# Three tiles' state-space output, gate and norm moved into the last attention blocks of an encoder-layer kernel

## The chip, the cores and the metric

The kernel runs on one core of a Trainium2 chip: one TensorE (PE), one VectorE (DVE), one ScalarE (ACT), one GpSimd (POOL), and DMA queues that are issued from SyncE (SP). Each engine works off its own queue in order and waits on semaphores for the others. The metric is the device time of one execution in microseconds (us), as the median of the runs.

## The reference

One layer of a hybrid encoder over a prompt of 2048 tokens and a sample of 256, model width 1024, fp32. What the change touches is the mixing of the two groups of heads:

```python
h = rms_norm(x, attn_norm_g)
q_lat, kv_lat, z, xbc, dt_raw = jnp.split(h @ w_in, IN_SPLITS, axis=-1)
mla_out = rms_norm(mla_mixer(q_lat, kv_lat, ...), attn_out_norm_g)   # 8 heads of attention, width 512
...
y = y_fwd + y_bwd + xs * d_skip                    # SSD: forward and backward chunked scan
y = y.reshape(b, s, SSD_WIDTH) * jax.nn.silu(z)    # gate, width 512
ssd_out = rms_norm(y, ssd_norm_g)
...
x = x + jnp.concatenate([mla_out, ssd_out], axis=-1) @ w_out
h = rms_norm(x, ffn_norm_g)
return x + (jax.nn.silu(h @ w_gate) * (h @ w_up)) @ w_down
```

## The kernel before

The tokens lie in 18 tiles of 128: tiles 0 to 15 are the prompt, 16 and 17 the sample. fp32 products are made of three matmuls with values split into a high and a low part: `mm3` (L115 to L117). A split takes two operations: the high part on ScalarE or GpSimd (weights: L123 or L121; banks: L130), the low part on VectorE (L126, L131).

The stages follow each other: input projections, conv and SSD scans (up to some 676 us), attention (to some 1549), output projection with the norms (`gather`, `turned`, `project`, to some 1800), a feed-forward part with up and gate, and the down projection.

Attention goes through a list `work` of blocks: 8 heads, and in each head the prompt's four blocks of 4 query tiles and one block of the sample. A block makes scores for its query tiles (L115 to L117), row maxima (`tensor_reduce`, L739, and L767 over the chunks) and exponentials (L748), and puts its key tiles on a list `turn`. While the next block makes its scores, these key tiles are turned (four transposes, L781, into a bank of the ring `ta`, `ta`, `tb`), split from the bank to SBUF (`pT`, L130 and L131) and multiplied with v (L789, L790). The block's result is turned back (L796, L808, L810, L811) and scaled into `mla` on GpSimd (L812). PE, ACT, DVE and POOL keep the order in which the code is written here (`manual_schedule`). After the last block only its remaining key tiles are left, the tail. Keys and values of even heads lie in pool `c_kv0`, of odd heads in `c_kv1`; SyncE's loads are ordered by the scheduler.

The output projection then goes through the tiles in falling order, 15 to 0, then 17, 16. `gather` adds the backward scan's state to the SSD output: state scaled on GpSimd (L896), summed on VectorE (L897), two matmuls (L902), product with the decay (L904), sum on GpSimd (L905); for the last tile of a sequence this falls away. Then come the gate (L908), two squares on ScalarE (L911, L912), a `rsqrt` of eleven small dependent operations on VectorE (L141 to L146) and two scalings (L914, L915). `turned` turns the tile (L923) and splits it (`mT`, L130, L131); `project` multiplies it with the eight output weights `wo0` to `wo7`, which are loaded and split (`load_wo`) at the third tile.

## Time and profile before

| | |
|---|---|
| median of 3 runs | 3298.39 us (3298.23 to 3300.56) |
| profiled execution | 3295.84 us, its span 3294.1 us |
| mean granted TensorE clock | 0.987 |
| busy share of the span | TensorE 97%, VectorE 71%, ScalarE 52%, GpSimd 9% |

A row of a timeline gives the start and the length of a run of equal instructions; the bracket at its end is the time in which the engine stood idle ahead of it, and what ended that. The ends of matmuls are modelled and overlap; the distance between two starts is the safer measure. The granted clock of 1.00 is 2.4 GHz, 0.50 is 1.2 GHz, and what lies between is a window with both.

### The profile page before, as it was taken

Reading aid. Unit: us, or ns where it says so; the run is one execution under the profiler, and the core shown is the slowest. Engines: PE = TensorE matmul, PEld = TensorE weight load, DVE = VectorE, ACT = ScalarE, POOL = GpSimd, SP = SyncE. Lnnn points to the kernel's source line nnn. Section 1 sums busy time; section 2 is a strip of 40 time slices with the busy share of each in tenths; the row PEclk is TensorE's granted clock in tenths of the full one; section 3 lists DMA queues with packets and bytes.
Section 4 is the critical chain, followed back from the end, with each engine's and each line's share of the span. In section 5 each row is a group of like instructions: output and inputs, shape, how many; then the busy total and the mean of one; then the engine's idle time right before and its main releaser. Section 6 shows DMA issues by size and latency. Waiting matters only on the chain.

```text
span 3294.1 us, 48707 instructions
## 1 busy us (share of the span) xinstructions
PE 3198.0 (97%) x17834; PEld 2855.6 (87%) x17834; DVE 2330.8 (71%) x4390; ACT 1707.7 (52%) x3578; POOL 306.9 (9%) x382
## 2 busy tenths in 40 slices
PE   7999999889999999998999999999999999999998
PEld 6888999878888888886788999999999999788887
DVE  5545677778888888888684777787778776344576
ACT  5454554567777777776322455445444444322233
POOL 2121133411111110001120000000000000000000
PEclk9999999999999999999999999999999999999999
DMA  8556422423323332102453333333333333554664
GB/s 299 206 203 205 154 103 101 125 78 92 87 64 89 94 87 61 45 20 86 132 170 121 110 132 125 144 110 127 127 143 107 121 123 123 159 154 151 185 194 138
DMA packets 263823, 419.43 MB, mean 127 GB/s; under 512 B 23392, under 2 KB 175744, under 8 KB 260960
## 3 DMA queue, kind: packets, MB, share of 16 engines
q1 hardware_dynamic: 263584, 416.31, 38.3%
q8 instruction: 141, 2.31, 0.3%
q14 instruction: 98, 0.80, 0.1%
HBM read 274.57 MB, written 145.65 MB: 128 GB/s over the span
## 4 chain that ended last, share of the span: by engine, by line
PE 81%; DVE 4%; DMA 2%; ACT 2%; issue 1%; POOL 0%; ACTq 0%; DVEq 0%; SPq 0%
PE bank_mb L1073 8%; PE bank_ma L1073 8%; PE bank_ta L1073 8%; PE bank_ma L117 7%; PE bank_ma L115 7%; PE bank_ma L116 7%; PE bank_mb L115 5%; PE bank_mb L117 5%; PE bank_mb L116 5%; PE bank_ta L781 4%; PE bank_o L789 3%; PE bank_o L790 3%; PE bank_tb L781 2%; PE bank_tb L1073 2%; PE bank_o L1073 2%; DVE Y L470 1%
## 5 line engine op out<-in xcount | busy, mean ns | idle before, releaser
L1006 DVE TENSOR_TENSOR ws<-rawf,ws 128x512 fp32r<-128x512 f32 x396 | 267.7, 688 | 100.5 <-ACT ws L1005 98.8
L1005 ACT ACTIVATE ws<-rawf 128x512 fp32r<-128x512 f32 x396 | 241.9, 627 | 178.4 <-PE bank_tb L1073 38.1
L1073 PE MATMUL bank_mb<-U,ws 128*128 128x384 f32 x1584 | 303.0, 336 | 2.3 <-ACT c L1082 2.2
L1073 PE MATMUL bank_ma<-U,ws 128*128 128x384 f32 x1584 | 300.8, 337 | 2.6 <-ACT U L1005 2.1
L1073 PE MATMUL bank_ta<-U,ws 128*128 128x384 f32 x1584 | 297.8, 335 | 3.7 <-ACT U L1005 2.4
L131 DVE TENSOR_TENSOR pT<-bank_ta,pT 128x512 fp32r<-128x512 f32 (+1 forms) x352 | 239.6, 681 | 62.3 <-ACT pT L130 52.5
L1073 PEld LDWEIGHTS bank_ta<-U,ws 128*128 128x128 f32 x1584 | 276.5, 188 | 5.4 <-ACT U L1005 2.9
L1073 PEld LDWEIGHTS bank_ma<-U,ws 128*128 128x128 f32 x1584 | 277.4, 189 | 3.6 <-ACT U L1005 2.4
L1073 PEld LDWEIGHTS bank_mb<-U,ws 128*128 128x128 f32 x1584 | 276.2, 188 | 4.0 <-ACT c L1082 3.9
L130 ACT ACTIVATE pT<-bank_ta 128x512 fp32r<-128x512 f32 (+1 forms) x352 | 209.1, 596 | 117.3 <-PE bank_ta L781 116.6
L789 PE MATMUL bank_o<-pT,v 128*128 128x512 f32 x528 | 249.5, 473 | 1.9 <-ACT ot L796 1.9
L781 PEld LDWEIGHTS bank_ta<-ident,pr 128*128 128x128 f32 x1388 | 171.4, 141 | 48.6 <-DVE pT L131 7.7
L781 PE MATMUL bank_ta<-ident,pr 128*128 128x128 f32 x1388 | 211.2, 274 | 2.0 <-DVE pT L131 2.0
L739 DVE TENSOR_REDUCE mx<-bank_ma 128x1 f32<-128x512 f32 (+1 forms) x261 | 177.0, 678 | 50.4 <-PE bank_ma L117 50.0
L790 PE MATMUL bank_o<-pT,v 128*128 128x512 f32 x528 | 206.8, 392 | 0.0
L1194 ACT ACTIVATE as<-rawa 128x1408 fp32r<-128x1408 f32 x63 | 86.9, 1379 | 225.2 <-PE bank_ma L117 118.1
L470 DVE SCALAR_TENSOR_TENSOR Y<-X,cw,Y 128x256 f32<-128x256 f32 x288 | 172.6, 661 | 27.6 <-ACT X L457 27.3
L748 ACT ACTIVATE pr<-bank_mb,mx 128x512 f32<-128x512 f32 (+1 forms) x261 | 181.4, 695 | 8.4 <-DVE mx L739 4.8
L748 ACT ACTIVATE pr<-bank_ma,mx 128x512 f32<-128x512 f32 (+1 forms) x261 | 179.1, 686 | 6.0 <-DVE mx L767 5.1
L739 DVE TENSOR_REDUCE mx<-bank_mb 128x1 f32<-128x512 f32 (+1 forms) x261 | 176.8, 677 | 7.2 <-PE bank_mb L117 3.6
L115 PE MATMUL bank_ma<-hT,wx 128*128 128x256 f32 x576 | 163.2, 284 | 2.1 <-POOL wx L121 1.5
L116 PE MATMUL bank_ma<-hT,wx 128*128 128x256 f32 x576 | 162.7, 283 | 0.0
...
## 6 DMA issues: line engine op xcount, KB each, us to landing
...
```

The lines of the kernel that those rows point to most:

```text
L115: nc.tensor.matmul(ps, wh, xh, start=start, stop=False)
L116: nc.tensor.matmul(ps, wh, xl, start=False, stop=False)
L117: nc.tensor.matmul(ps, wl, xh, start=False, stop=stop)
L131: nc.vector.tensor_tensor(lo, ps, f(hi), op=ALU.subtract)
L739: nc.vector.tensor_reduce(mx[:, j:j + 1], ps[:, :m * P], axis=AX.X, op=ALU.max, negate=nch == 1)
L748: nc.scalar.activation(e[:, :m * P], ps[:, :m * P], AF.Exp, bias=bias, accum_out=rs[:, i, j:j + 1])
L781: nc.tensor.transpose(ps[:, i * P:(i + 1) * P], pr[i, kt // 4][:, kt % 4 * P:(kt % 4 + 1) * P], ident)
L789: nc.tensor.matmul(po[0][:, :n], v[:, s0 + kt, :], pT[:, 0, :n], start=kt == 0, stop=False)
L790: nc.tensor.matmul(po[0][:, :n], v[:, s0 + kt, :], pT[:, 1, :n], start=False, stop=kt == sn - 1)
L1005: nc.scalar.activation(dst[:, 0], src, AF.Copy)
L1006: nc.vector.tensor_tensor(dst[:, 1], src, f(dst)[:, 0], op=ALU.subtract)
L1073: nc.tensor.matmul(ps[:, :W], w[:, a, k, :], x[:, b, k, :], start=k + n == 0 and not more, stop=k == HK - 1 and n == 2, skip_group_check=more)
```

## The change

- The blocks of the last head are worked off backwards: prompt tiles 12 to 15 first, then 8, 4 and 0, then the sample's block.
- `gather` is cut in two: `ssd_out` (SSD output, gate and its square) and `gather` (attention's square, rsqrt, two scalings). For tiles 15, 14 and 13 both stand in attention's code: `ssd_out` of 15 after block 4, of 14 after block 0 with `gather` of 15 behind it, of 13 after the sample's block with `gather` of 14 and 13 behind it. Then follow the tail's key tiles.
- Their buffers, and those of all later tiles, are slices of the tiles that held the even heads' keys and values (`mixk`, `mixv`), since the last head is an odd one. There are 3 y, 2 z, 2 state terms, 2 states (before: 4, 2, 3, 2). A unit of the output matmuls goes to a bank of the ring `t` instead of `o`.
- `wo0` is loaded and split when three blocks are left. `wo1` to `wo7` are loaded ahead of the projection's loop, which begins at its third step.
- The pool `c_kv0` and two small ones are opened ahead of attention's other pools.

The diff, without blank lines and without the body of the old `gather` (its operations are those of `ssd_out` and `gather`):

```diff
                 nc.sync.dma_start(d_B[m][:, j], out)
+    G = 3
+    W = G * P
+    assert NT % (2 * G) == 0
+    order = [c for c, _ in falling(1)]
+    parts = [(order[i:i + G], order[i + G:i + 2 * G]) for i in range(0, NT, 2 * G)]
+    kv0 = pool(mixer, "c_kv0", 1)
+    small = pool(mixer, "d_s", 2)
+    w0p = pool(mixer, "d_w0", 1)
+    ends = {a + m - 1 for a, m in seq_tiles}
+    bst, wo, mix = {}, {}, {}
+    def load_wo(k, home):
+        wo[k] = home.tile([P, 2, D], F32R, name=f"wo{k}")
+        raw = op.tile([P, D], F32, name="o", tag="o")
+        nc.sync.dma_start(raw, io["w_out"][:, k, :])
+        split_w(wo[k][:, 0], wo[k][:, 1], raw, "pool" if k % 2 else "act")
+    def mix_tiles():
+        a = kv0.tile([P, 9, SW], F32, name="mixk", tag="k")
+        b = kv0.tile([P, NT * P], F32, name="mixv", tag="v")
+        mix["y"], mix["z"], mix["sc"] = ([a[:, i, :] for i in r] for r in ((0, 1, 2), (3, 4), (5, 6)))
+        mix["g"] = a[:, 7], a[:, 8]
+        mix["nsb"], mix["to"] = ([b[:, i * SW:(i + 1) * SW] for i in r] for r in ((0, 1), (2,)))
+        mix["ct"] = [b[:, 3 * SW + i * NG * P:3 * SW + (i + 1) * NG * P] for i in range(2)]
+        nc.sync.dma_start(mix["g"][0], io["mix_g"][:, :SW].to_broadcast([P, SW]))
+        nc.sync.dma_start(mix["g"][1], io["mix_g"][:, SW:].to_broadcast([P, SW]))
+    def nxt(name):
+        mix[name].append(mix[name].pop(0))
+        return mix[name][-1]
+    def hbd(a, c):
+        return a[:, 1, c, :].rearrange("p (h o) -> p h o", o=1).to_broadcast([P, SH, SP])
+    def by_head(a):
+        return a.rearrange("p (h d) -> p h d", h=SH)
+    def ssd_out(c):
+        y, z, sc = nxt("y"), nxt("z"), nxt("sc")
+        nc.sync.dma_start(y, d_y[c])
+        nc.sync.dma_start(z, d_z[c])
+        nc.sync.dma_start(sc, d_sb[c])
+        if c not in ends:
+            ct = nxt("ct")
+            nc.sync.dma_start(ct, d_C[c])
+            old = bst["s"]
+            ns = nxt("nsb")
+            nc.gpsimd.tensor_tensor(by_head(ns), by_head(old), hbd(dec, c), op=ALU.mult)
+            nc.vector.tensor_tensor(ns, ns, sc, op=ALU.add)
+            bst["s"] = ns
+            po = bank("t")
+            for g in range(NG):
+                s = slice(g * 256, (g + 1) * 256)
+                nc.tensor.matmul(po[:, s], ct[:, g * P:(g + 1) * P], old[:, s], start=True, stop=True)
+            to = nxt("to")
+            nc.vector.tensor_tensor(by_head(to), by_head(po), hbd(dfs, c), op=ALU.mult)
+            nc.gpsimd.tensor_tensor(y, y, to, op=ALU.add)
+        else:
+            bst["s"] = sc
+        nc.vector.tensor_tensor(y, y, z, op=ALU.mult)
+        ss = small.tile([P, 16], F32, name="ss2", tag="ss2")
+        nc.scalar.activation(z, y, AF.Square, accum_out=ss[:, 1:2])
+        return y, z, ss
+    def gather(c, y, z, ss):
+        nc.scalar.activation(z, mla[c][:, 0, :], AF.Square, accum_out=ss[:, 0:1])
+        r = rsqrt(small, ss[:, :2], 2, SW, "m")
+        nc.vector.scalar_tensor_tensor(mla[c][:, 0, :], mla[c][:, 0, :], r[:, 0:1], mix["g"][0], op0=ALU.mult, op1=ALU.mult)
+        nc.vector.scalar_tensor_tensor(y, y, r[:, 1:2], mix["g"][1], op0=ALU.mult, op1=ALU.mult)
+        return y
     with ExitStack() as ph:
-        kvs = [pool(ph, "c_kv0", 1)]
+        kvs = [kv0]
         qp = pool(ph, "c_q", 2)
         lp = pool(ph, "c_l", 2)
         sb = pool(ph, "c_sb", 2)
@@ -814,7 +891,8 @@
             for kt in range(sn):
                 turn.append(lambda kt=kt: turned(kt))
-        work = [(h, s0 + o, min(4, sn - o), s0, sn) for h in range(NH) for s0, sn in seq_tiles for o in range(0, sn, 4)]
+        work = [(h, s0 + o, min(4, sn - o), s0, sn) for h in range(NH) for s0, sn in seq_tiles for o in list(range(0, sn, 4))[::-1 if h == NH - 1 else 1]]
         heads = {}
         def next_block():
@@ -826,24 +904,29 @@
         next_block()
         sums = block_sums()
         with tc.manual_schedule(engines={mybir.EngineType.PE, mybir.EngineType.Activation, mybir.EngineType.DVE, mybir.EngineType.Pool}):
+            ys = {}
             while work:
                 next_block()
                 for _ in range(2):
                     next(sums, None)
-            for _ in sums:
-                pass
+                if len(work) == 3:
+                    for _ in sums:
+                        pass
+                    mix_tiles()
+                    load_wo(0, w0p)
+                if len(work) < 3:
+                    ys[2 - len(work)] = ssd_out(order[2 - len(work)])
+                if len(work) == 1:
+                    ys[0] = gather(order[0], *ys[0])
+            for i in (1, 2):
+                ys[i] = gather(order[i], *ys[i])
             while tail:
                 tail.popleft()()
             while turn or prod or late:
                 step()
-    G = 3
-    W = G * P
-    assert NT % (2 * G) == 0
-    order = [c for c, _ in falling(1)]
-    parts = [(order[i:i + G], order[i + G:i + 2 * G]) for i in range(0, NT, 2 * G)]
     hbs = [pool(ctx, "e_hb0", 1, side="right")]
     H, first_xs = {}, {}
@@ -861,59 +944,6 @@
         sb = pool(ph, "d_sb", 2)
         wp = pool(ph, "d_w", 1)
         mp = pool(ph, "d_m", 2)
-        wo = [wp.tile([P, 2, D], F32R, name=f"wo{k}") for k in range(KD)]
-        def load_wo(k):
-            raw = op.tile([P, D], F32, name="o", tag="o")
-            nc.sync.dma_start(raw, io["w_out"][:, k, :])
-            split_w(wo[k][:, 0], wo[k][:, 1], raw, "pool" if k % 2 else "act")
-        grow = wp.tile([P, D], F32, name="grow")
-        nc.sync.dma_start(grow, io["mix_g"].to_broadcast([P, D]))
...
         def turned(c, y):
             mT = mp.tile([P, 2, KD, P], F32R, name="mT", tag="mT", bufs=3)
@@ -944,13 +974,12 @@
             if c == order[G]:
                 columns_of(0, 0, [first_xs.pop(t) for t in order[:G]])
-        ys, mTs = {}, {}
-        WO = {2: range(KD)}
-        for i in range(NT + 3):
-            if i < NT:
-                ys[i] = gather(order[i])
-            for k in WO.get(i, ()):
-                load_wo(k)
+        mTs = {}
+        for k in range(1, KD):
+            load_wo(k, wp)
+        for i in range(2, NT + 3):
+            if 2 < i < NT:
+                ys[i] = gather(order[i], *ssd_out(order[i]))
             if 0 <= i - 2 < NT:
                 mTs[i - 2] = turned(order[i - 2], ys.pop(i - 2))
             if 0 <= i - 3 < NT:
```

How it moves instructions, at three places. In the changed kernel L816 is the reduction of scores, L858 the transposes of key tiles, L866 and L867 the products, L888 the turning back, L738, L740, L744 the output matmuls, decay product and gate, L753 and L754 the scalings, L953 the transposes of `turned`.

VectorE, before, in attention's last key tiles (`nsb` is the state of the scan):

```order
L131 TENSOR_TENSOR pT<-bank_ta,pT 128x512
L897 TENSOR_TENSOR nsb<-nsb,sc 128x512
L131 TENSOR_TENSOR pT<-bank_ta,pT 128x512
L802 TENSOR_REDUCE ri<-rs 128x4
L803 RECIPROCAL ri<-ri 128x4
L811 TENSOR_TENSOR lo<-bank_tb,lo 128x256
L131 TENSOR_TENSOR pT<-bank_ta,pT 128x512
L897 TENSOR_TENSOR nsb<-nsb,sc 128x512
```

VectorE in the changed kernel, at the same place: the step with `ssd_out` of tile 14 and `gather` of tile 15.

```order
L131 TENSOR_TENSOR pT<-bank_tb,pT 128x512
L131 TENSOR_TENSOR pT<-bank_ta,pT 128x512
L733 TENSOR_TENSOR mixv<-mixv,mixk 128x512
L740 TENSOR_TENSOR mixv<-bank_tb,dfs 128x512
L744 TENSOR_TENSOR mixk<-mixk 128x512
L141 TENSOR_SCALAR rs_ms<-ss_16956 128x2
...
L144 SCALAR_TENSOR_TENSOR rs_u<-rs_y 128x2
L145 TENSOR_TENSOR rs_u<-rs_u,rs_ms 128x2
L146 SCALAR_TENSOR_TENSOR rs_y<-rs_u,rs_y 128x2
L753 SCALAR_TENSOR_TENSOR mla_7376<-mla_7376,rs_y,mixk 128x512
L754 SCALAR_TENSOR_TENSOR mixk<-mixk,rs_y 128x512
L816 TENSOR_REDUCE mx<-bank_ma 128x1
L131 TENSOR_TENSOR pT<-bank_ta,pT 128x512 x3
```

Eleven small operations (three are shown ahead of the scalings), a decay product, a gate and two scalings now stand in one piece between the split of one key tile and that of the next.

VectorE, before, a few rows after attention's last product, where the first gates and weight splits stand (`wo_17501` is `wo0`, the next are `wo1` to `wo3`):

```order
L908 TENSOR_TENSOR y_17538<-y_17538,z_17539 128x512
L144 SCALAR_TENSOR_TENSOR rs_u<-rs_y 128x2
L904 TENSOR_TENSOR to_17590<-bank_o,dfs 128x512
L145 TENSOR_TENSOR rs_u<-rs_u,rs_ms 128x2
L897 TENSOR_TENSOR nsb<-nsb,sc 128x512
L126 TENSOR_TENSOR wo_17501<-o,wo_17501 128x1024
L146 SCALAR_TENSOR_TENSOR rs_y<-rs_u,rs_y 128x2
L126 TENSOR_TENSOR wo_17502<-o,wo_17502 128x1024
L126 TENSOR_TENSOR wo_17503<-o,wo_17503 128x1024
L126 TENSOR_TENSOR wo_17504<-o,wo_17504 128x1024
```

VectorE in the changed kernel, after attention's last product (`wo_17600` is `wo1`, then `wo2`, `wo4`, `wo3`):

```order
L888 TENSOR_TENSOR lo<-bank_tb,lo 128x256
L882 RECIPROCAL ri<-rs 128x2
L888 TENSOR_TENSOR lo<-bank_ta,lo 128x128
L740 TENSOR_TENSOR mixv<-bank_ta,dfs 128x512
L126 TENSOR_TENSOR wo_17600<-o,wo_17600 128x1024
L126 TENSOR_TENSOR wo_17605<-o,wo_17605 128x1024
L126 TENSOR_TENSOR wo_17615<-o,wo_17615 128x1024
L126 TENSOR_TENSOR wo_17610<-o,wo_17610 128x1024
L131 TENSOR_TENSOR mT<-bank_ta,mT 128x512
L131 TENSOR_TENSOR mT<-bank_tb,mT 128x512
```

Four weight splits now stand in a row ahead of the first split of `mT`, and the gates and rsqrt of the first tiles are gone from here.

TensorE, before, at the end of the SSD part (L588 updates states, L601 makes diagonal outputs; the rows with k and q are scores of attention's first block):

```order
L115 MATMUL bank_mb<-k,q 128x512
L116 MATMUL bank_mb<-k,q 128x512
L117 MATMUL bank_mb<-k,q 128x512
L588 MATMUL bank_tb<-xd_7214,bt 128x256 x2
L115 MATMUL bank_ta<-k,q 128x512
...
L588 MATMUL bank_tb<-xd_7285,bt 128x256 x2
L601 MATMUL bank_o<-xs,e_7248 128x64 x7
L580 MATMUL bank_tb<-ns_7291,Y 128x256 x2
L588 MATMUL bank_tb<-xd_7326,bt 128x256 x2
L588 MATMUL bank_tb<-xd_7328,bt 128x256 x2
L115 MATMUL bank_tb<-k,q 128x512
```

TensorE in the changed kernel, at the same place:

```order
L588 MATMUL bank_tb<-xd_7214,bt 128x256 x2
L601 MATMUL bank_o<-xs,e_7165 128x64 x8
L588 MATMUL bank_tb<-xd_7216,bt 128x256 x2
L588 MATMUL bank_tb<-xd_7283,bt 128x256 x2
L601 MATMUL bank_o<-xs,e_7248 128x64
L588 MATMUL bank_tb<-xd_7285,bt 128x256 x2
L601 MATMUL bank_o<-xs,e_7248 128x64 x7
L580 MATMUL bank_tb<-ns_7291,Y 128x256 x2
L588 MATMUL bank_tb<-xd_7326,bt 128x256 x2
L588 MATMUL bank_tb<-xd_7328,bt 128x256 x2
L115 MATMUL bank_ma<-k,q 128x512
L116 MATMUL bank_ma<-k,q 128x512
```

The score groups that stood between the SSD part's matmuls now stand behind the last of them. On SyncE's queue the first q load moved likewise from ahead of the last stores of the scan to behind `d_sb_168`.

## Rows read from the trace of the kernel before

**Rows 1.** The page's busy time of each engine over the whole span: us, share of the span, instructions.

```profile
PE 3198.0 (97%) x17834; PEld 2855.6 (87%) x17834; DVE 2330.8 (71%) x4390; ACT 1707.7 (52%) x3578; POOL 306.9 (9%) x382
```

**Rows 2.** Windows by stage, core 0: start and end, length, then busy us (instructions) of TensorE, its weight loads, VectorE, ScalarE and GpSimd, the granted clock, the DMA share and GB/s. Attention ends shortly before 1550; the output projection fills 1600 to 1700.

```profile
1400.00:1500.00 100.00, 99.27 (x562) 81.24 (x561) 82.90 (x151) 76.90 (x193) 2.85 (x5) 1.00 0.06 17
1530.00:1540.00 10.00, 8.76 (x58) 7.03 (x57) 8.78 (x17) 7.97 (x20) 1.66 (x2) 1.00 0.36 120
1550.00:1560.00 10.00, 4.15 (x14) 2.41 (x12) 9.00 (x15) 4.37 (x10) 7.00 (x8) 0.75 0.51 159
1560.00:1570.00 10.00, 2.05 (x5) 1.18 (x5) 9.88 (x17) 2.39 (x5) 4.33 (x4) 0.50 0.99 350
1570.00:1580.00 10.00, 7.89 (x24) 5.87 (x25) 10.00 (x17) 3.36 (x7) 4.14 (x4) 0.55 0.36 112
1590.00:1600.00 10.00, 8.97 (x44) 6.94 (x43) 9.90 (x35) 3.93 (x10) 3.06 (x3) 1.00 0.57 172
1600.00:1700.00 100.00, 100.00 (x488) 83.81 (x487) 69.95 (x206) 26.85 (x58) 14.61 (x12) 1.00 0.45 147
```

**Rows 3.** Timeline of TensorE at the join of attention and output projection: start, us, instruction, and in brackets the idle time ahead of it and what ended that.

```profile
1549.07 1.07 PE L808 MATMUL bank_ta<-ident,ot 128*128 128x128 f32 x6
1549.98 1.03 PE L902 MATMUL bank_o<-sc,ct 128*128 128x256 f32 x4
...
1557.85 2.04 PE L902 MATMUL bank_o<-nsb,ct 128*128 128x256 f32 x4 [4.91 <-DVE rs_u L145]
1567.29 2.05 PE L902 MATMUL bank_o<-nsb,ct 128*128 128x256 f32 x4 [7.39 <-DVE rs_u L144]
1570.00 1.11 PE L923 MATMUL bank_tb<-ident,mla 128*128 128x128 f32 x4 [0.66 <-DVE mla L914]
...
1572.28 0.78 PE L115 MATMUL bank_ma<-wo,mT 128*128 128x512 f32 x1
...
1577.50 0.99 PE L117 MATMUL bank_ma<-wo,mT 128*128 128x512 f32 x1
...
1579.27 0.39 PE L115 MATMUL bank_ma<-wo,mT 128*128 128x512 f32 x1
```

**Rows 4.** Timeline of VectorE at the same join.

```profile
1551.05 0.69 DVE L904 TENSOR_TENSOR to<-bank_o,dfs 128x512 f32<-128x512 f32 x1 [0.37 <-PE bank_o L902]
1551.66 0.28 DVE L811 TENSOR_TENSOR lo<-bank_ta,lo 128x128 f32<-128x128 f32 x1
...
1553.51 0.96 DVE L144 SCALAR_TENSOR_TENSOR rs_u<-rs_y 128x2 f32<-128x2 f32 x1
...
1556.40 0.68 DVE L908 TENSOR_TENSOR y<-y,z 128x512 f32<-128x512 f32 x1
...
1558.34 2.29 DVE L126 TENSOR_TENSOR wo<-o,wo 128x1024 fp32r<-128x1024 f32 x1
...
1561.47 3.48 DVE L126 TENSOR_TENSOR wo<-o,wo 128x1024 fp32r<-128x1024 f32 x3
```

**Rows 5.** Timeline of VectorE a little later, with GpSimd idle from 1590.5: the end of one rsqrt and the two scalings behind it.

```profile
1590.55 0.16 DVE L144 SCALAR_TENSOR_TENSOR rs_u<-rs_y 128x2 f32<-128x2 f32 x1
1590.74 0.16 DVE L145 TENSOR_TENSOR rs_u<-rs_u,rs_ms 128x2 f32<-128x2 f32 x1
...
1591.14 0.75 DVE L914 SCALAR_TENSOR_TENSOR mla<-mla,rs_y,grow 128x512 f32<-128x512 f32 x1
1591.81 0.75 DVE L915 SCALAR_TENSOR_TENSOR y<-y,rs_y,grow 128x512 f32<-128x512 f32 x1
```

**Rows 6.** Timeline of ScalarE at the join: the two squares of one tile.

```profile
1565.79 0.63 ACT L911 ACTIVATE junk<-y 128x512 f32<-128x512 f32 x1 [7.14 <-DVE y L908]
...
1566.54 0.63 ACT L912 ACTIVATE junk<-mla 128x512 f32<-128x512 f32 x1
```

**Rows 7.** Timeline of GpSimd at the join.

```profile
1551.82 1.27 POOL L905 TENSOR_TENSOR y<-y,to 128x512 f32<-128x512 f32 x1 [0.52 <-DVE to L904]
...
1553.41 1.04 POOL L896 TENSOR_TENSOR nsb<-nsb,dec 128x512 f32<-128x512 f32 x1
1554.43 2.04 POOL L121 TENSOR_SCALAR wo<-o 128x1024 fp32r<-128x1024 f32 x2
```

**Rows 8.** Timeline of VectorE in attention's last key tiles.

```profile
1543.00 0.69 DVE L131 TENSOR_TENSOR pT<-bank_ta,pT 128x512 fp32r<-128x512 f32 x1 [0.21 <-ACT pT L130]
```

**Rows 9.** Timeline of TensorE from the end of the SSD part into attention.

```profile
674.72 1.10 PE L588 MATMUL bank_tb<-xd,bt 128*128 128x256 f32 x4 [0.94 <-DVE ns L592]
...
680.28 0.50 PE L115 MATMUL bank_ma<-k,q 96*128 96x512 f32 x1 [2.76 <-ACT pr L748]
...
681.39 0.63 PE L116 MATMUL bank_mb<-k,q 96*128 96x512 f32 x1
...
684.73 0.40 PE L115 MATMUL bank_ta<-k,q 96*128 96x512 f32 x1
684.97 0.40 PE L116 MATMUL bank_ta<-k,q 96*128 96x512 f32 x1
```

**Rows 10.** Timeline of VectorE in the same place: the first of the seven reductions and the row maximum.

```profile
675.09 0.68 DVE L739 TENSOR_REDUCE mx<-bank_ma 128x1 f32<-128x512 f32 x1
...
679.27 0.14 DVE L767 TENSOR_REDUCE mx<-mx 128x1 f32<-128x4 f32 x1
```

**Rows 11.** Timeline of SyncE's queue there: the store that waits.

```profile
666.24 4.16 SPq L598 DMA_DIRECT2D d_sb<-ns  x2
```

39 lines of the change are left out of this document (removed).

## The prediction

> **What bounds the kernel now.** I read the page's busy time first: TensorE is busy for 97% of the span [rows 1], so a change pays only where TensorE stands idle. The windows by stage then say where that is around the change [rows 2]: attention keeps TensorE at 99 of 100 us, the output projection at 100 of 100, and the one big hole is the join of the two, 4.15, 2.05 and 7.89 us busy in the three windows from 1550 to 1580. In those windows VectorE is busy for 9.0 to 10.0 of 10 us and the granted clock is 0.75, 0.50 and 0.55. TensorE's own timeline shows the same [rows 3]: attention's last transposes (L808) start at 1549.07, the SSD output matmuls (L902) wait 4.91 and 7.39 us for VectorE, and steady projection begins with L117 at 1577.50. So the join takes 1577.5 - 1549.1 = 28.4 us. In it TensorE does work that must be done in any case: five L902 steps of 0.86 us, two groups of transposes (L923) of 0.43, four matmuls with the first output weight of 0.24, together 6.1 us at full clock. VectorE's rows name the rest [rows 4]: eight splits of output weights (L126, 1.16 us each where three ran alone, 2.29 beside GpSimd), gate and norm of the first tiles.
>
> **The change, part by part.** It moves three tiles' gate and norm and one of the eight splits ahead of the join. I count a loss ahead of it and a gain in it, with E the start of attention's last transposes.
>
> *Start of attention.* Other pools are opened, and the first q load now stands on SyncE's queue behind a store that waited until 666.24 + 4.16 = 670.4 [rows 11]. So all seven first score groups stand behind the SSD part's last matmuls (L588, 674.72) where before five stood ahead of them. Before, the seven reductions ran back to back from 675.09 and the row maximum was ready at 679.27 + 0.14 = 679.4 [rows 10]. Now: last L588 about 675.6, seven groups of three matmuls at 0.70 us (3 x 0.235, the spacing from 684.73 to 684.97) [rows 9] = 4.9, a reduction 0.68, the maximum 0.2: 681.3. **+1.9 us**; 0 if the SSD part ends earlier without the score groups in its midst, +4 if q lands late.
>
> *First step in the tail (tile 14's output, gathers 15).* What counts is that VectorE's queue is in order: the whole step stands in front of the L131 which empties the bank that TensorE's next transposes write. From the end of the SSD output matmuls: product with the decay 0.69 (L904's row) [rows 4]; GpSimd adds, 1.27 [rows 7]; gate 0.68 [rows 4]; two squares on ScalarE, 0.75 apart, 1.4 [rows 6]; eleven dependent operations of rsqrt, 0.19 apart where GpSimd is idle, 2.1, and two scalings of 0.67, 1.33 [rows 5]; some 0.4 for four hand-overs between engines; one reduction and the L131 itself, 0.9. Sum 8.8. TensorE has a score group of half width and one key tile to do meanwhile (0.35 + 0.90; the tail's period is 0.69 busy and 0.21 idle on VectorE [rows 8]). **Stall 7.5 us.**
>
> *Second step (tile 13's output, gathers 14 and 13).* After the matmuls GpSimd first scales the next state (1.04) and then adds (1.27) [rows 7]; gate 0.68, two squares 1.4, two chains of 2.1 + 1.33, hand-overs 0.4, L131 0.6, and VectorE's state sum fits beside GpSimd: 12.2. TensorE has two key tiles and a group of transposes, 2.2. **Stall 10.0 us.** Bounds for both: VectorE's own work alone (GpSimd and ScalarE ahead of it) gives 4 + 7 = 11; GpSimd beside VectorE through the gate and the state sums adds up to 1 each, 19.5.
>
> *What the stalls do to the clock.* After 7.39 us of waiting TensorE ran at a granted clock of 0.50 to 0.55, the lower of its levels, 1.2 GHz [rows 2, 3]. After 2.76 us at the start of attention eight matmuls from 681.39 to 684.73 took 3.34 us instead of 8 x 0.235 = 1.88 [rows 9]. I take 1.6 us after each stall: **+3.2**, from 0 to 5. The Trainium skill ("TensorE: Matmul & The Clock Gate", section "HAM oscillation") says that a kernel which leaves TensorE idle between bursts pays the lower clock anew after each gap; by it the one hole becomes three, and without that term the sum below would be 6 instead of 9. The trace agrees with 0.50 and 0.55 after the waits.
>
> *Work now in the tail.* Two SSD output steps, 1.7 us. The first, for tile 15, has only gate and one square: covered by VectorE's 0.21 idle per key tile. So is the first weight's split (1.16 on VectorE), but for up to 1 us. Against these stands an idle 1.24 us in 1530 to 1540, which goes, as its state sums are now inside the steps: **+0.5** for the three.
>
> E moves by 1.9 + 17.5 + 3.2 + 0.5 = **23.1 us**.
>
> *The join after.* VectorE's row is two L888 (the second ended at 1551.66 + 0.28 before, 2.9 us after E) [rows 4], a decay product 0.69, four splits (the first waits for GpSimd's, 1.02 [rows 7], which stands behind its last scaling into mla; one runs beside GpSimd's next, 2.29; three of 1.16, together 5.8), and only then the L131 of tile 15's second half-row, for which the next transposes and the matmuls with the first weight wait. 2.9 + 0.7 + 1.0 + 5.8 + 0.7 + 0.4 = 11.5 us from E to steady projection; 9 if no split meets GpSimd, 14 if two do. Instead of 28.4: **-16.9**. But TensorE has then done only 3.4 us (three output steps, two of them counted in the tail, and two groups of transposes): **+2.7** owed. Gaps behind: 2.3 us before (1.03 idle in 1590 to 1600, the rest the lower clock), 2.7 after: **+0.4**.
>
> *Later stages.* Fewer buffers (y 3, sc 2) serve the projection, where TensorE is busy 100 of 100 us [rows 2] and a tile takes it 48 matmuls of 0.24 [rows 9], 11 us. Nothing can be gained there; no row shows what fewer buffers cost, and I take 0 since 11 us leave room for the loads, with up to 5 in the range. The feed-forward part has the same rows of instructions: 0. The output weights 5 to 7 are wanted some 8 us after steady projection begins; they are loaded by then: 0.
>
> **Sum:** +23.1 - 16.9 + 2.7 + 0.4 = +9.3 us. The profiled execution took 3295.84 us (span 3294.1), so 3305.1 for such a run. It lies 2.5 us below the median of the runs, 3298.39, from which the prediction goes: **3307.7 us**.
>
> **The rivals.**
>
> *The tail hides the steps (faster).* In the tail VectorE idles 0.21 of each 0.90 us [rows 8], and the steps add only about 4 and 7 us of VectorE's own work; if TensorE finds other work while they run, the 17.5 and the 3.2 fall away. The sum is then 9.3 - 20.7 = -11.4: 3287. It decides from the point where both stalls and the clock cost under 5 us together. Against it: the order puts each step in one piece between two L131, and the transposes turn over three banks only, so TensorE runs dry within two key tiles. Chance 0.18, with other sums that end there.
>
> *Loss and gain cancel (same).* The stalls fall to VectorE's own work (11 us instead of 17.5) since GpSimd and ScalarE run ahead, and start and clock cost half: 9.3 - 6.5 - 1 - 1.6 = +0.2: 3298.6. For it: GpSimd's scaling of the state needs nothing of the tail. Against it: the add needs the product, which needs the matmuls, so 1.27 and 1.4 cannot run ahead. Chance 0.27.
>
> *GpSimd beside the chains (slower yet).* With GpSimd busy the small operations took 0.96 instead of 0.16 [rows 4, 5]. If its scaling falls into one of the three rsqrt chains, that chain grows by 11 x 0.8 = 9 us, and the time is 3317. The queue of GpSimd holds nothing for those moments, so chance 0.06. The Trainium skill ("GPSIMD Engine Reference", section "Specifications") says that GpSimd shares its SBUF interfaces with VectorE and disturbs operations with two SBUF inputs or in a two-port mode; by it the gate (two SBUF inputs) beside GpSimd's scaling in the first step would cost up to twice, and the sum would be 10 instead of 9. The trace shows 2.29 instead of 1.16 for L126.
>
> **How the numbers follow.** The forecast, some 6 to 16 us slower, has 0.49. A measurement of this kernel can tell about 0.2%, 6.6 us, from no change: same is 3291.8 to 3305.0. Slower 0.49 + 0.06 = 0.55, same 0.27, faster 0.18. The forecast's own range is 3305 to 3316. The bounds of the terms (start 0 to 4, stalls 11 to 19.5, clock 0 to 5, join 9 to 14) reach, two at a time, from about 3293 to 3317; with the third rival and a part of the first the range is 3290 to 3319, and some 0.2 is left out.
>
> **What would show it.** In the changed kernel's profile: two waits of TensorE of 7 to 10 us for VectorE's L131 ahead of attention's end, each followed by matmuls at the lower clock; between them small operations 0.19 apart; attention's first exponential at 681; four L126 in a row at the join, and steady projection 11 us after the last transposes. I am wrong if the tail shows no wait above 4 us, or if the join is longer than 14 us (then a load is late), or if TensorE idles between 1620 and 1800.

## The result and the profile after

| | before | after |
|---|---|---|
| median of 4 runs each, us | 3299.41 (3298.23 to 3300.56) | 3319.36 (3314.74 to 3324.90) |
| ratio | | 1.0065, interval 1.0053 to 1.0077 |
| profiled execution, us (span) | 3295.84 (3294.1) | 3318.43 (3316.5) |

The change makes the kernel 20 us slower, where 9.3 were forecast: the sign was right, the size less than half. Four more runs of the changed kernel, unedited, gave a median of 3324.07 beside 3297.38 (ratio 1.0076, 1.0059 to 1.0093), with one execution at 3313.74 and three at 3322 to 3326. The profile of that 3313.74 is the second one used below. Two executions of the experiments lie far above all others, one of e5 at 12367.52 us and one of e6 at 4251.41 us (the profiled one, so that e6 was run once more), and stand in none of the medians.

To see where the time went I laid the timelines of before and after beside each other at marks that both have: the n-th row maximum of attention (L767 before, L844 after, counted from 0), the last `lo` sum (L811, L888), the last of the projection's 36 additions, and the sums that begin the feed-forward products (L1051, L1080). The differences between marks are the stages:

| stage, us against the profile of before | forecast | after | after, second profile |
|---|---|---|---|
| start, and attention up to row maximum 119 | +1.9 | +4.4 | +0.2 |
| row maximum 119 to 120 (first weight's split) | 0 | +2.2 | +2.2 |
| on to row maximum 127 | 0 | +0.1 | +0.1 |
| from there to attention's end (two steps, tail) | +21.2 | +24.6 | +23.7 |
| attention's end to projection's end (join) | -13.8 | -15.6 | -15.8 |
| feed-forward part | 0 | +6.7 | +7.5 |
| sum (span) | +9.3 | +22.4 | +17.9 |

The windows of after, with the columns of [rows 2]:

```profile
1530.00:1540.00 10.00, 7.00 (x43) 5.70 (x41) 7.32 (x11) 4.94 (x13) 2.27 (x2) 0.98 0.19 66
1540.00:1550.00 10.00, 4.56 (x18) 4.10 (x19) 6.25 (x19) 4.57 (x14) 0.00 (x0) 0.50 0.08 28
1550.00:1560.00 10.00, 3.91 (x25) 3.15 (x23) 6.79 (x18) 4.30 (x12) 2.26 (x2) 0.84 0.40 116
1560.00:1570.00 10.00, 4.91 (x18) 4.21 (x19) 7.20 (x22) 1.53 (x3) 0.61 (x1) 0.50 0.01 2
1570.00:1580.00 10.00, 9.31 (x57) 7.42 (x56) 6.54 (x12) 5.81 (x11) 0.00 (x0) 0.98 0.00 0
1580.00:1590.00 10.00, 6.23 (x34) 4.21 (x33) 6.32 (x7) 4.50 (x8) 7.21 (x6) 1.00 0.55 187
1590.00:1600.00 10.00, 7.21 (x21) 5.69 (x22) 9.63 (x12) 2.50 (x5) 2.59 (x2) 0.66 0.50 170
1600.00:1630.00 30.00, 30.00 (x144) 25.08 (x143) 23.74 (x77) 7.74 (x17) 4.59 (x4) 1.00 0.44 140
```

The one hole of before has become three: 1537 to 1545, 1554 to 1565, 1588 to 1593. In the first two VectorE is busy for 5.75 of 8.40 us and for 8.98 of 11.20 us, no other engine for more than half: VectorE's own queue makes up most of them, and its waits for GpSimd and ScalarE, 2.8 and 2.1 us, the rest. TensorE's timeline of after names the waits, as [rows 3] did:

```profile
1545.44 1.09 PE L858 MATMUL bank_ta<-ident,pr 128*128 128x128 f32 x4 [8.44 <-DVE pT L131]
1546.18 0.78 PE L866 MATMUL bank_o<-pT,v 128*128 128x512 f32 x1
...
1550.09 0.48 PE L866 MATMUL bank_o<-pT,v 128*128 128x512 f32 x1
...
1565.10 1.12 PE L858 MATMUL bank_tb<-ident,pr 128*128 128x128 f32 x4 [11.19 <-DVE pT L131]
...
1580.38 0.60 PE L885 MATMUL bank_tb<-ident,ot 128*128 128x128 f32 x4
...
1592.79 0.80 PE L117 MATMUL bank_ma<-wo,mT 128*128 128x512 f32 x1 [4.99 <-DVE mT L131]
```

Behind the first wait a product (L866) takes 0.78 until 1550, then 0.48: the lower of the two clock levels (1.2 GHz) for some 4.6 us; behind the second for some 5.2. VectorE's timeline (compare [rows 4, 5 and 8]) shows what stood ahead of those two L131:

```profile
1537.87 1.51 DVE L744 TENSOR_TENSOR mixk<-mixk 128x512 f32<-128x512 f32 x1 [1.38 <-POOL mixk L741]
1540.78 0.17 DVE L141 TENSOR_SCALAR rs_ms<-ss 128x2 f32<-128x2 f32 x1 [1.40 <-ACT mixk L751]
1540.98 0.17 DVE L142 TENSOR_SCALAR rs_y<-rs_ms 128x2 int32<-128x2 int32 x1
...
1542.95 0.75 DVE L753 SCALAR_TENSOR_TENSOR mla<-mla,rs_y,mixk 128x512 f32<-128x512 f32 x1
1543.62 0.75 DVE L754 SCALAR_TENSOR_TENSOR mixk<-mixk,rs_y 128x512 f32<-128x512 f32 x1
1544.28 0.42 DVE L816 TENSOR_REDUCE mx<-bank_ma 128x1 f32<-128x256 f32 x1
1544.61 1.28 DVE L131 TENSOR_TENSOR pT<-bank_ta,pT 128x512 fp32r<-128x512 f32 x2
...
1553.57 1.74 DVE L733 TENSOR_TENSOR mixv<-mixv,mixk 128x512 f32<-128x512 f32 x1 [0.62 <-POOL mixv L732]
...
1585.08 7.06 DVE L126 TENSOR_TENSOR wo<-o,wo 128x1024 fp32r<-128x1024 f32 x4
1592.06 0.68 DVE L131 TENSOR_TENSOR mT<-bank_ta,mT 128x512 fp32r<-128x512 f32 x1
```

The first step is read downwards: the gate waits 1.38 for GpSimd's add, lasts 1.51, then VectorE waits 1.40 for ScalarE's squares, makes eleven small operations 0.195 apart, two scalings, a reduction, and only then the L131 that TensorE wants. The last two rows are the join: four splits in a row, then `mT`. GpSimd's row for the gate's 1.51 (0.68 in [rows 4]) and for the sum's 1.74:

```profile
1537.79 1.04 POOL L732 TENSOR_TENSOR mixv<-mixv,dec 128x512 f32<-128x512 f32 x1
...
1553.49 1.26 POOL L741 TENSOR_TENSOR mixk<-mixk,mixv 128x512 f32<-128x512 f32 x1
```

### The profile page after: what moved, and what is told of

The parts are those of the page before. It is cut to its first block, busy times and chain, and to the rows that moved or that the text cites. A ratio compares the mean times of both kernels' runs of the same rounds, so it can differ in the third digit from the quotient of the medians.

```text
span 3316.5 us, 48684 instructions
## 1 busy us (share of the span) xinstructions
PE 3204.7 (97%) x17834; PEld 2859.6 (86%) x17834; DVE 2332.3 (70%) x4390; ACT 1707.5 (51%) x3578; POOL 303.5 (9%) x382
## 4 chain that ended last, share of the span: by engine, by line
PE 71%; DVE 4%; ACT 2%; DMA 1%; issue 1%; POOL 0%; ACTq 0%; DVEq 0%
PE bank_ma L1102 8%; PE bank_mb L1102 8%; PE bank_ta L1102 8%; PE bank_ma L117 5%; PE bank_ma L115 5%; PE bank_ma L116 5%; PE bank_mb L115 5%; PE bank_mb L117 5%; PE bank_mb L116 5%; PE bank_ta L858 4%; PE bank_o L866 3%; PE bank_o L867 3%; PE bank_tb L858 2%; PE bank_tb L1102 2%; PE bank_o L1102 2%
## 5 line engine op out<-in xcount | busy, mean ns | idle before, releaser
L1034 ACT ACTIVATE ws<-rawf 128x512 fp32r<-128x512 f32 x396 | 241.8, 627 | 179.8 <-PE bank_ta L1102 37.3
L131 DVE TENSOR_TENSOR pT<-bank_ta,pT 128x512 fp32r<-128x512 f32 (+1 forms) x352 | 239.3, 680 | 66.1 <-ACT pT L130 56.9
L866 PE MATMUL bank_o<-pT,v 128*128 128x512 f32 x528 | 250.6, 475 | 0.7 <-ACT ot L873 0.7
L858 PE MATMUL bank_ta<-ident,pr 128*128 128x128 f32 x1386 | 212.4, 275 | 10.9 <-DVE pT L131 10.4
L858 PEld LDWEIGHTS bank_ta<-ident,pr 128*128 128x128 f32 x1386 | 171.9, 141 | 58.8 <-issue 9.4
L816 DVE TENSOR_REDUCE mx<-bank_ma 128x1 f32<-128x512 f32 (+1 forms) x261 | 177.1, 678 | 50.4 <-PE bank_ma L117 49.9
L867 PE MATMUL bank_o<-pT,v 128*128 128x512 f32 x528 | 207.8, 394 | 0.0
L816 DVE TENSOR_REDUCE mx<-bank_mb 128x1 f32<-128x512 f32 (+1 forms) x261 | 176.9, 678 | 7.3 <-PE bank_mb L117 3.8
```

The source lines that it names most:

```text
L131: nc.vector.tensor_tensor(lo, ps, f(hi), op=ALU.subtract)
L816: nc.vector.tensor_reduce(mx[:, j:j + 1], ps[:, :m * P], axis=AX.X, op=ALU.max, negate=nch == 1)
L858: nc.tensor.transpose(ps[:, i * P:(i + 1) * P], pr[i, kt // 4][:, kt % 4 * P:(kt % 4 + 1) * P], ident)
L866: nc.tensor.matmul(po[0][:, :n], v[:, s0 + kt, :], pT[:, 0, :n], start=kt == 0, stop=False)
L867: nc.tensor.matmul(po[0][:, :n], v[:, s0 + kt, :], pT[:, 1, :n], start=False, stop=kt == sn - 1)
L1034: nc.scalar.activation(dst[:, 0], src, AF.Copy)
```

## The experiments

Each kernel ran beside runs of the kernel before on the same chip. The shifts of the marks in the profile of each against the profile of before, us (attention's row maxima by number; "end" is the last `lo` sum; "FF 6" and "FF 26" are sums of the feed-forward part):

| kernel | row 0 | 119 | 120 | 127 | end | projection's end | FF 6 | FF 26 | span |
|---|---|---|---|---|---|---|---|---|---|
| after | 2.8 | 4.4 | 6.6 | 6.7 | 31.3 | 15.7 | 18.0 | 21.5 | 22.4 |
| after_again | 0.9 | 0.2 | 2.4 | 2.5 | 26.2 | 10.4 | 12.6 | 16.1 | 17.9 |
| e1_pools | 12.3 | 13.8 | 13.9 | 13.9 | 13.9 | 12.9 | 12.9 | 12.5 | 12.5 |
| e1_again | 14.1 | 15.2 | 15.2 | 15.2 | 15.2 | 16.6 | 17.4 | 17.1 | 17.6 |
| e2_behind | 14.6 | 15.2 | 17.5 | 17.4 | 17.4 | 13.3 | 14.6 | 14.7 | 12.7 |
| e3_reverse | -0.5 | 0.4 | 0.4 | 0.5 | 1.3 | -4.3 | -3.2 | -3.3 | -1.9 |
| e4_spread | 13.9 | 14.5 | 16.7 | 24.2 | 25.9 | 10.5 | 12.6 | 13.8 | 13.7 |
| e5_nopools | 0.9 | 0.1 | 0.1 | 0.4 | 24.2 | 8.2 | 10.2 | 10.8 | 10.0 |
| e6_again | -2.9 | -2.0 | -2.0 | 4.1 | 5.7 | -10.1 | -8.4 | -8.0 | -8.6 |
| d1_dose | 0.9 | -0.1 | -0.1 | 0.2 | 20.5 | 4.6 | 6.7 | 9.4 | 7.8 |
| d2_scale | -0.8 | -0.8 | -0.8 | -0.5 | 25.0 | 9.5 | 11.4 | 11.8 | 9.5 |
| d3_wolate | 9.7 | 11.4 | 11.5 | 11.6 | 36.6 | 21.4 | 23.2 | 23.9 | 21.2 |

**e1: the kernel before, with only the two small pools opened.**

```diff
-        kvs = [pool(ph, "c_kv0", 1)]
+        kv0 = pool(ph, "c_kv0", 1)
+        small = pool(ph, "d_s", 2)
+        w0p = pool(ph, "d_w0", 1)
...
+        kvs = [kv0]
```

> The kernel before with nothing changed but the pools: the even heads' key pool and two small ones are opened ahead of attention's other pools, as in the changed kernel (the small ones stay unused). If the late start of attention in the changed kernel (its first row maximum came at 682.1 instead of 679.3, and some 3.7 us were lost by the end of the first block) is the work of the pools' places, this kernel is slower than before by 3 to 4 us. If it comes from anything else in the change, it takes the time of the kernel before within 1 us.

Measured 3307.90 beside 3298.03 (1.0025, 1.0015 to 1.0036; eight runs from 3300.76 to 3310.93): +9.9, although these buffers hold nothing that is used. All of it is there at the first row maximum. TensorE's timeline at the end of the SSD part shows why, beside [rows 9]; e1 first, then after:

```profile
672.30 2.04 PE L588 MATMUL bank_tb<-xd,bt 128*128 128x256 f32 x4 [0.46 <-ACT ns L594]
674.14 3.08 PE L601 MATMUL bank_o<-xs,e 128*128 128x64 f32 x14
...
679.91 2.04 PE L588 MATMUL bank_tb<-xd,bt 128*128 128x256 f32 x4 [0.88 <-DVE to L582]
```

```profile
669.01 1.08 PE L588 MATMUL bank_tb<-xd,bt 128*128 128x256 f32 x4
669.93 1.67 PE L601 MATMUL bank_o<-xs,e 128*128 128x64 f32 x14
...
673.40 1.10 PE L588 MATMUL bank_tb<-xd,bt 128*128 128x256 f32 x4 [0.88 <-DVE to L582]
```

The same matmuls take 2.04 and 3.08 instead of 1.10 and 1.67. The windows 670 to 680 of e1 and of after:

```profile
670.00:680.00 10.00, 8.67 (x29) 6.81 (x27) 1.77 (x2) 1.19 (x2) 3.24 (x4) 0.50 0.44 130
```

```profile
670.00:680.00 10.00, 8.18 (x43) 6.54 (x42) 4.67 (x7) 1.19 (x2) 2.85 (x3) 1.00 0.51 159
```

In e1 the granted clock is 0.50, and 29 instructions of TensorE fit where in after 43 do. The score groups that before stood between the SSD part's matmuls are gone from there in both. TensorE's instructions are the same, in the same order, up to there in all kernels with these pools; the five profiles of e1 (two), e2, e4 and d3 show 0.50 in this window, the two of after 1.00. In the six profiles of kernels without the pools, whose score groups stand at their old places, the windows 660 to 665 and 665 to 670 show 1.00. So the pools bring the low clock, but not always; that it is the missing filler which does so is argued from this and was not tried apart. The times of e2 and e4 fall in two groups, as they would if the level differed from execution to execution: seven of e2 from 3305.2 to 3308.7 and two at 3296.5 and 3298.4, six of e4 from 3307.5 to 3309.6 and four from 3298.6 to 3302.9. Those of e1 do not part so clearly. The three runs of after_again at 3322 to 3326, 8.5 to 12.4 above its profiled one, report a mean clock of 0.982 to 0.983 against 0.987; that these three had the low clock at this place is inferred, not seen.

**e1_again: e1, unedited, once more.**

> The kernel before with attention's pools displaced, unedited, looked at once more. Theory as for the changed kernel: either 12 to 14 us late at the first row maximum, with matmuls of the state update (L588) at 2.0 us, or 3 to 4 us late, with the same matmuls at 1.1 us. Rival: some third place of the late start, with the same clock in both.

3313.51 in one execution; L588 again at 2.04, the shift at the first row maximum 14.1.

**e2: the three steps behind attention's last key tile.**

```diff
-                if len(work) < 3:
-                    ys[2 - len(work)] = ssd_out(order[2 - len(work)])
...
-            for i in (1, 2):
-                ys[i] = gather(order[i], *ys[i])
             while turn or prod or late:
                 step()
+            for i in range(G):
+                ys[i] = ssd_out(order[i])
+                ys[i] = gather(order[i], *ys[i])
```

> The changed kernel with the output, gate and norm of its first three tiles put behind attention's last key tile instead of among them; all else as in the changed kernel. Theory (VectorE's in-order queue held TensorE up in the tail): the tail's two waits of 8.4 and 11.2 us go, attention ends some 25 us earlier, and the three tiles' chains, some 21 us in a row, now stand in the join, which grows from 12 to about 33 us: 4 to 9 us less than the changed kernel, 3310 to 3315. Rival (the loss is that of the late start and of the later stages, the tail matters little): no gain or a loss against the changed kernel of up to 10 us, 3319 to 3330.

3305.94 beside 3298.03 (1.0022, 1.0012 to 1.0031), under the range expected. With the steps gone from it, the tail costs nothing (17.4 at row 127, 17.4 at the end), and the join gives 4.1 instead of 15.6: TensorE waits there 16.13 us in one piece. The 4.1 is near what the reversed blocks alone give there (5.6 in e3). The steps thus cost 24.6 us in the tail, and save 11.5 at the join by being gone from it.

**e3: the kernel before, with only the last head's blocks backwards.**

```diff
-        work = [(h, s0 + o, min(4, sn - o), s0, sn) for h in range(NH) for s0, sn in seq_tiles for o in range(0, sn, 4)]
+        work = [(h, s0 + o, min(4, sn - o), s0, sn) for h in range(NH) for s0, sn in seq_tiles for o in list(range(0, sn, 4))[::-1 if h == NH - 1 else 1]]
```

> The kernel before with nothing changed but the order of the last head's blocks (backwards). Theory: the order of blocks costs nothing, within 1 us of the kernel before. Rival: the other order of the last blocks costs a part of the 2.2 us that the changed kernel lost between its first and its second last block, so 1 to 3 us slower.

3292.14 beside 3298.03 (0.9984, 0.9975 to 0.9994): 5.9 faster, where neither theory expected a gain. From attention's end to the projection's end the shift falls by 5.6. TensorE's rows at its join:

```profile
1553.15 1.10 PE L902 MATMUL bank_o<-nsb,ct 128*128 128x256 f32 x4 [0.83 <-POOL mla L812]
...
1556.01 1.10 PE L902 MATMUL bank_o<-nsb,ct 128*128 128x256 f32 x4 [1.76 <-DVE to L904]
...
1564.63 1.11 PE L923 MATMUL bank_tb<-ident,mla 128*128 128x128 f32 x4 [7.52 <-DVE mla L914]
```

Where [rows 3] had waits of 4.91, 7.39 and 0.66, there are now 0.83, 1.76 and 7.52: one long wait less. That tile 15's attention is ready earlier, so that its norm need not wait, is my reading of it and was not tried apart.

**e4: the same operations in some 38 pieces, one behind each key tile of the last three blocks.**

```diff
+    def early(ys):
+        for stage in ("out0", "out1", "norm0", "norm1", "out2", "norm2"):
...
         def step(hold=False):
             more = bool(turn)
+            next(spread[0], None)
...
-                if len(work) < 3:
-                    ys[2 - len(work)] = ssd_out(order[2 - len(work)])
...
+                    spread[0] = early(ys)
```

> The changed kernel with the same operations for the first three tiles, cut into some 38 pieces and begun two blocks earlier: one piece after each key tile of the last three blocks, in place of three pieces. Theory (what cost 19.6 us is that each step stood in one piece in front of the next split of a key tile): no wait of TensorE above 2 us is left in the tail, attention ends at most 8 us later than in the kernel before, and the join keeps its gain of some 15 us: 3291 to 3300, so 20 to 28 us below the changed kernel. Rival (VectorE has no room for 13 us more in attention, wherever they stand): TensorE loses about the same in many small waits, 3310 to 3320.

3307.55 beside 3298.03 (1.0023, 1.0014 to 1.0033): missed, but by the start alone (13.9 in its profile). From row 120 to the end it loses 9.2 instead of 24.7, and the join gives 15.4.

**e5: the changed kernel without the small pools, the first weight loaded with the others.**

```diff
-    small = pool(mixer, "d_s", 2)
-    w0p = pool(mixer, "d_w0", 1)
...
-                    load_wo(0, w0p)
...
-        for k in range(1, KD):
+        for k in range(KD):
```

> The changed kernel without the two small pools ahead of attention's pools: the small tiles lie in what is left of the even heads' value tile, and the first output weight is loaded with the other seven; the steps in the tail stay as they are. The order of TensorE's queue up to attention's last blocks is then that of the kernel before. Theory (the late start is the small pools' work, the 2.2 us between the first and the second last block are the early weight's split, the rest is the tail's): attention starts with the kernel before, the tail still costs some 25 us, the join gains some 14: 10 to 16 us above the kernel before, so below the changed kernel. Rival (the start costs little, and tail and later stages make up the whole): no better than the changed kernel, 18 us or more above the kernel before.

3306.95 beside 3297.38 (1.0026, 1.0016 to 1.0035): +9.6. The start and the step at row 120 are gone (0.9 and 0.0), the tail's 23.8 and the join's 16.0 stay.

**e6: spread, without pools, the first weight late** (the edits of e4 and e5 together).

> The spread kernel (the three tiles' operations in 38 pieces, one after each key tile) without the two small pools and with the first output weight loaded late. Theory: the start is that of the kernel before, the spread pieces cost some 7 us in attention's last two blocks, the join gains 14: 1 to 6 us below the kernel before. Rival (spreading only moves the loss to where VectorE is fuller): at least 3 us above the kernel before.

3288.93 beside 3297.38 (0.9972, 0.9959 to 0.9984): 8.4 us under the kernel before, and well under the changed one.

> The spread version once more, for its trace: the three tiles' steps in some 38 pieces, one behind each key tile of the last three blocks, no small pools, the first output weight with the others. Theory (in pieces the steps need no wait of TensorE of over 2 us, the start is that of the kernel before, and the join is as short as in the changed kernel): 5 to 10 us below the kernel before, no shift up to attention's last blocks, +7 to +9 in attention's last three blocks and tail together, -15 at the join, and, as in each kernel whose steps have left the last phase, +1.7 where the feed-forward part begins. Rival (its earlier time came from something else than the tail): waits of over 4 us stand in the tail and the gain is of another stage.

3289.69 beside 3297.86 (0.9975, 0.9966 to 0.9985), 8.2 under the kernel before. Its windows and its longest waits up to the join:

```profile
1530.00:1540.00 10.00, 7.45 (x47) 5.50 (x46) 7.40 (x23) 8.84 (x25) 0.00 (x0) 1.00 0.09 28
1540.00:1550.00 10.00, 9.90 (x66) 8.21 (x67) 8.52 (x16) 6.13 (x12) 0.61 (x1) 1.00 0.00 0
```

```profile
1535.85 0.63 PE L930 MATMUL bank_ta<-ident,pr 128*128 128x128 f32 x4 [1.06 <-DVE mixv L819]
1539.87 0.51 PE L938 MATMUL bank_o<-pT,v 128*128 128x512 f32 x1 [1.24 <-ACT ot L945]
...
1567.26 0.80 PE L117 MATMUL bank_ma<-wo,mT 128*128 128x512 f32 x1 [2.77 <-DVE mT L131]
```

No wait of the tail is over 1.24 us and the clock stays at 1.00; from row 119 to the end the pieces cost 7.7 us, and the join gives 15.8. Not all of the 8.2 is the moved work's: reversing the blocks alone (e3) gave 5.9, and the profile of e6 is already 2.0 ahead at row 119. From there to the projection's end e6 gains 8.1 and e3 4.7, so the three tiles' work in pieces is worth some 3 us.

**after_again: the changed kernel, unedited.**

> The changed kernel itself, unedited, beside the others on one chip. Theory: the end of the SSD part, without the score groups in its midst, runs in some executions at TensorE's full clock (start of attention 3 to 4 us late) and in others at half (12 to 14 us late); so this kernel's times spread over some 10 us, from 3314 to 3326, and a profile shows one of the two. Rival: the spread has another place, and the start is 3 to 4 us late in every execution.

3324.07 beside 3297.38; its profile is the second one of the result.

**d1: one pass of the reciprocal root instead of three in the first three tiles, on e5.**

```diff
-        for _ in range(3):
+        for _ in range(1 if pool is None and len(early) < 3 else 3):
```

> The changed kernel without its two small pools and with the first output weight loaded at its old place (as e5), and with one pass of the reciprocal root in place of three in the first three tiles' norms, so that their roots are less exact. It takes six of eleven small operations out of each chain, 6 x 0.195 = 1.2 us in the first stall and two chains or 2.3 us in the second. Theory (TensorE's waits in the tail are the length of VectorE's queue ahead of the turned copies): the waits fall from 8.42 and 10.61 to 7.2 and 8.3, the stretch from the tail's entry to attention's end from +23.8 to about +20.3, the time by 3.5, from 9.6 above the kernel before to about 6. Rival (the end of each wait is set by ScalarE's squares or GpSimd's sums, beside which the small operations lie): the waits and the time stay within 1 us of those of e5.

3303.74 beside 3297.86 (1.0017, 1.0007 to 1.0026): +5.9, 3.7 less than e5. TensorE's two waits in e5 and in d1:

```profile
1539.10 1.09 PE L862 MATMUL bank_ta<-ident,pr 128*128 128x128 f32 x4 [8.42 <-DVE pT L131]
...
1558.96 1.11 PE L862 MATMUL bank_tb<-ident,pr 128*128 128x128 f32 x4 [10.61 <-DVE pT L131]
```

```profile
1537.73 1.08 PE L865 MATMUL bank_ta<-ident,pr 128*128 128x128 f32 x4 [7.24 <-DVE pT L131]
...
1554.80 1.12 PE L865 MATMUL bank_tb<-ident,pr 128*128 128x128 f32 x4 [8.81 <-DVE pT L131]
```

They fall by 1.18 (1.17 worked out) and 1.80 (2.3 worked out), the tail by 3.5 (23.8 to 20.3). Small operations of 0.16 us on VectorE are paid for in TensorE's time: one for one in the first stall, for some three quarters in the second.

**d2: the state scaling of two tiles on VectorE instead of GpSimd, on e5.**

```diff
-            nc.gpsimd.tensor_tensor(by_head(ns), by_head(old), hbd(dec, c), op=ALU.mult)
+            (nc.vector if c in order[:3] else nc.gpsimd).tensor_tensor(by_head(ns), by_head(old), hbd(dec, c), op=ALU.mult)
```

> As e5, with the scaling of the SSD state of the second and third tile on VectorE in place of GpSimd. Theory (a VectorE operation of 128x512 beside a GpSimd one takes 1.5 to 1.7 us where it takes 0.68 alone): the gate of the second tile, which ran beside GpSimd's scaling in 1.52, falls to 0.7, the first stall from 8.42 to about 7.6 or, as the scaling is queued there too, stays within 0.3 of it; in the second step the sum no longer waits 0.62 for GpSimd, but the scaling takes 0.7 and one of the two still lies beside GpSimd's add at 1.5 to 1.7: the second stall changes by less than 0.5. The time by less than 1.5 either way. Rival (the 1.52 and 1.74 are of these operations or of their operands, whatever GpSimd does): the gate stays at 1.5 and the first stall grows by the scaling's 0.7.

3305.45 beside 3297.86 (1.0025, 1.0015 to 1.0036). The gate of the first step, 1.52 in e5:

```profile
1531.29 0.69 DVE L748 TENSOR_TENSOR mixk<-mixk 128x512 f32<-128x512 f32 x1 [1.38 <-POOL mixk L745]
```

So the 0.83 was GpSimd's presence, not the operation's. The first stall is 8.28 instead of 8.42, as the scaling's 0.68 is queued in its place; the second grows by 0.77 to 11.38 (under 0.5 was expected), where a scaling of 0.68 is queued too and the fourth tile's sum still lasts 1.73 beside GpSimd's add.

**d3: the changed kernel, pools kept, only the first weight's load and split moved back.**

```diff
-                    load_wo(0, w0p)
...
-        for k in range(1, KD):
-            load_wo(k, wp)
+        for k in range(KD):
+            load_wo(k, wp if k else w0p)
```

> The changed kernel, both small pools kept, with only the load and split of the first output weight moved back to where the others are. Theory (the split of that weight on ScalarE and VectorE is on the path inside attention): the step of 2.2 us between attention's row maxima 119 and 120 goes (under 0.3), and the steady projection begins some 0 to 1 us later behind attention's end, as one more weight is split there. Rival (the step is of the loads that the change issues at that place): it stays at 2.2. The scan's tail is as in the changed kernel, so the start lies anywhere from -1 to +14.

3317.09 in one execution. The step from row 119 to 120 is 0.0 instead of 2.2. In after, VectorE's timeline there reads:

```profile
1482.07 1.23 DVE L126 TENSOR_TENSOR wo<-o,wo 128x1024 fp32r<-128x1024 f32 x1 [1.59 <-ACT wo L123]
```

VectorE waits 1.59 for ScalarE's half of the split and works 1.23 on its own; both stand in the queue ahead of the score reductions.

## Why the prediction was right in sign and wrong in size

The profiled execution of the result, 3318.43, lies near the median of 3319.36, and its sum is 22.4 where 9.3 was forecast. Of the 13.1 between them, 6.7 is of the feed-forward part, 3.4 of stalls, clock and tail, 2.5 of the start and 2.2 of the first weight; the join gives 1.8 back. In the second profile 8.6 are missing: 7.5, 2.5, -1.7, 2.2 and -2.0. So the step that failed most, in both, is a stage put at nothing because its rows are the same.

**"The feed-forward part has the same rows of instructions: 0": the step that failed, +6.7 and +7.5.** The rows are the same, their waits are not. About 2 us are lost where it begins: TensorE waits there for the splits of U by L1034 3.93 and 4.51 us, before, by L1005, 2.09 and 2.36. Before first, then after:

```profile
1824.47 0.53 PE L1073 MATMUL bank_ma<-U,ws 128*128 128x384 f32 x1 [2.09 <-ACT U L1005]
1827.68 1.01 PE L1073 MATMUL bank_ta<-U,ws 128*128 128x384 f32 x2 [2.36 <-ACT U L1005]
```

```profile
1838.69 0.69 PE L1102 MATMUL bank_ma<-U,ws 128*128 128x384 f32 x1 [3.93 <-ACT U L1034]
1844.21 1.01 PE L1102 MATMUL bank_ta<-U,ws 128*128 128x384 f32 x2 [4.51 <-ACT U L1034]
```

All kernels in which the three steps left the projection's code lose 1.3 to 2.3 there; e1, e1_again and e3 lose 0 to 1.1. Then 3.5 us come at one place, about 2158, where VectorE waits for a load; the issue on SyncE's queue and the wait, before and after:

```profile
2132.82 1.47 SPq L1041 DMA_DIRECT2D rawf<-w_gu  x2
2138.03 0.69 DVE L1051 TENSOR_TENSOR S<-rawf 128x512 f32<-128x512 f32 x1 [0.64 <-DMA rawf<-w_gu]
```

```profile
2150.82 1.79 SPq L1070 DMA_DIRECT2D rawf<-w_gu  x2
2158.67 0.69 DVE L1080 TENSOR_TENSOR S<-rawf 128x512 f32<-128x512 f32 x1 [3.27 <-DMA rawf<-w_gu]
```

The load was issued 18.0 later, as all around it, so not late; but VectorE could begin 7.9 us behind the issue instead of 5.2. Both profiles of after have it, d1 has 2.7 us at that place, e4 1.2, the others under 1. Over the whole part the other kernels lie between -0.6 and +3.3, d3, whose code in this part is the same, at -0.2. Why the load takes longer stays open; so does the rest of the 6.7, and no profile shows the part in the executions that were not profiled.

**"+1.9 us; 0 if the SSD part ends earlier, +4 if q lands late" (start): right in the two profiles, wrong for the pools.** The prediction saw that five score groups leave the gaps of the SSD part, and priced only their being done later, with the SSD matmuls at their old 1.10. In the two profiles of after, whose clock stayed at 1.00, that was about right at the first row maximum (+2.8 and +0.9). It did not ask what TensorE's clock does where filler is taken out: the pools alone cost 9.9 us (median of e1), with L588 at 2.04 in both profiles of e1. For the executions of after at 3320 to 3326 such a start is inferred, not seen; there it would be the larger miss.

**"So is the first weight's split ... but for up to 1 us": 2.2.** It counted VectorE's 1.16 against VectorE's idle time, and left out that an in-order queue also waits for the operand: 1.59 for ScalarE. d3 shows the whole 2.2.

**The two stalls, 7.5 + 10.0: right in mechanism, 19.6 measured** (8.44 + 11.19). d1 shows that they follow the length of VectorE's queue, and e4 and e6, in which no such wait is left, that they go when it is broken up. What was short: the gate was taken at 0.68 and lasted 1.51 beside GpSimd's scaling (d2: 0.69 without it), and the fourth tile's state sum, said to fit beside GpSimd, lasted 1.74 beside its add. The gate ended 0.55 us after GpSimd's scaling, the sum 0.56 after its add. The rule of the Trainium skill ("GPSIMD Engine Reference", section "Specifications") on operations with two SBUF inputs thus held here, shown for the gate (1.52 in e5, 0.69 in d2) and read from the rows for the sum (1.74 against 0.68).

**The clock behind the stalls, 3.2: about 4.9.** Half speed lasts for 4.6 and 5.2 us, half of which is lost. It lay inside the bound of 5. The Trainium skill ("TensorE: Matmul & The Clock Gate", section "HAM oscillation") says that the lower clock is paid anew after each gap; the windows agree, with 0.50, 0.50 and 0.66 behind the three holes.

**The join, -16.9 + 2.7 + 0.4 = -13.8: right, -15.6.** Four L126 stood in a row, and steady projection began 12.4 us after the last transposes (11.5 forecast).

The medians add up as well: e5, which is the change without pools and early weight, is 9.6 above before (the forecast without its start term: 7.4), the pools alone 9.9, the early weight 2.2 in the profile: 21.7, against 20.0 and 26.7 measured in the two sets of runs. But the profiles of after divide that sum otherwise, with 4.4 and 0.2 at row 119 and some 5 us more than e5 in the feed-forward part, so the agreement is in part chance. So is that of e5 with its 7.4: its tail cost 23.8 instead of 21.2, its join gave 16.0 instead of 13.8, and its feed-forward part lost 1.8. The terms that the prediction worked out at length were each sized within some 3 us; the miss lies in what it priced in a sentence: buffers, one weight, and later stages.

Of the rivals, "the tail hides the steps" fell for this kernel, but e6 shows what it takes: the same work in pieces of one or two operations, 7.7 us instead of 24. "Loss and gain cancel" fell too: the stalls were 19.6, not 11. "GpSimd beside the chains" did not occur: all small operations stood 0.195 apart.
